# Gated-delta stage of a two-block network: the second chunk's decays and the work behind four value heads are traced one head later, and the transposes get two more PSUM banks

## The chip, the cores and the metric

The kernel runs on one core of a Trainium2 chip. The metric is the device time of one execution in microseconds (us), as the median over several runs. Beside it there is the profile of one execution, taken by the hardware profiler, whose rows are quoted below. Engines are named as in the profile: PE is the matrix engine (PEld its weight loads), DVE the vector engine, ACT the scalar engine, POOL the GpSimd engine, SP the queue that issues nearly all DMAs.

## The reference

The reference computes two blocks on 256 tokens of width 1024: a hybrid attention mixer with a product-key expert layer, and then a block of banded attention followed by a gated delta rule over 16 meta tokens and two chunks of 128 tokens. The change lies in the last part, which is this (cut to what matters):

```python
def deltanet_mixer(h, norm_w, w_in, conv_w, ...):
    u = rms_norm(h, norm_w) @ w_in
    qkv, z, b, a = split(u)
    qkv = silu(causal_depthwise_conv(qkv, conv_w))      # 4 taps
    q, k = l2_norm(...), l2_norm(...)                   # 8 key heads, 16 value heads
    beta, g = sigmoid(b), -exp(a_log) * softplus(a + dt_bias)
    o = chunked_gated_delta_rule(q, k, v, beta, g)
    return (rms_norm(o, o_norm_w) * silu(z)) @ w_out

def step(S, (qc, kc, vc, bc, gc)):                      # one chunk, per head
    gcum  = cumsum(gc)
    decay = exp(where(causal, gcum[:, None] - gcum[None, :], -inf))
    m     = where(strict, (kc * bc) @ kc.T * decay, 0)
    u, w  = solve(m + eye, [vc * bc, kc * bc * exp(gcum)])   # unit triangular
    v_new = u - w @ S
    o     = (qc * exp(gcum)) @ S + ((qc @ kc.T) * decay) @ v_new
    S     = S * exp(gcum[-1]) + (kc * exp(gcum[-1] - gcum)).T @ v_new
    return S, o
```

## The kernel before, in words

Everything is written for one core in a tile language. A scheduler takes the traced instructions and gives each engine a fixed list, in which it lets the earlier traced instruction go first among those that its own timeline holds ready; on the chip each engine then goes through its list from the front, and an instruction that waits holds back all behind it. Buffers of a pool are handed out in turn in the order of the trace: a tile that gets the buffer of an older one has to wait for the last reader of that one.

The delta stage (`delta`, from L1258) projects the input with 49 weight units of 128 x 1024. In this text they are numbered in order: unit 0 holds the gates b and a, units 1 to 8 the key heads, 9 to 16 the query heads, 17 to 32 the 16 value heads, 33 to 48 the 16 gate heads z. For each unit SP loads `raw` (L265, 4 buffers), ACT makes `hi` (L273, 3 buffers), DVE makes `lo` (L274, 3 buffers), and PE does 24 matmuls (L284 to L286) into `pj_ps`, a pool of two PSUM banks. So `hi` and `lo` of a unit need the buffers that PE frees when it is done with the unit three before, and PE's next unit needs a bank that ACT has read.

A head's convolution (`conv_head`, L1332) is two copies on ACT (`cpad`, and `craw` or `qT`: L1344, L1345) that free the bank, and three steps on DVE (L1356). Four value heads form one `raw` tile, called `craw` in the rows (2 buffers). When its four heads are done, ACT takes the SiLU of it (L1361), PE transposes it for the two chunks and for the meta tokens (`tp`, L1602, L1608, and the keys of the meta tokens L1613), ACT copies the results out (`v` L1604, `va` L1610, `ka` L1615), PE forms `mv` (L1618), DVE `vsA` (L1621), PE `mS`, and ACT the state `S` (L1626). All four `tp` banks of a group come from the pool `pb`, two banks, which `mv`, `mS` and the scores `kq` of `attend` use too. The tiles of z share the two buffers of `craw` (tag `craw`): the heads of the second z tile, units 37 to 40, are written over the last group's `raw`.

Two things run beside that. First the decays: for each chunk, `decay` sums the log decays on PE into four banks (`dec`, two from `pk` and two from `pb`), `between` adds the causal mask on PE (L1405) and takes 16 exponentials on ACT (L1409), DVE multiplies by the key products (`U`, L1500), and SP writes the 32 x 32 diagonal blocks of `U` to DRAM (`e1`, L1503). Second the inverse (`inverse`, a generator that `values` advances by one piece at each of its yields): SP reads all blocks back as 128 rows (`ab`, L1522), DVE solves them in 31 pairs of steps (`sb_t` L1253, `ub` L1255), SP writes the result (`e2`, L1527, named `e<-ub` in the rows) and reads it into the diagonal of `U` (L1530), and then, for each of 8 groups (2 chunks x 4 groups of heads), PE, ACT and DVE join the blocks in a chain: `r1` (L1550), `pr` on ACT (L1553), `zt` and `z1` (L1558, L1562), copies, `r2` (L1570), `rn` on ACT (L1573), `z2` (L1576). `zt` and `z2` use the two banks of `pk`, in turn.

After the last unit `step(0, h0)` and `step(1, h0)` run the recurrence itself, and `out` multiplies with the output weights.

Of the kernel before, what the change touches and what calls it, by code (L numbers as in the profile page):

```python
# [6 lines left out]
F32 = mybir.dt.float32  # L7
# [4 lines left out]
AF = mybir.ActivationFunctionType  # L12
ALU = mybir.AluOpType
# [5 lines left out]
M = 16  # L19
# [171 lines left out]
class Net:  # L191
# [1066 lines left out]
    def delta(self, NZ=2, AH=4, KN=8, SS=1, SR=3, SW=3):  # L1258
        nc, ap = self.nc, self.ap
        ident, tri = self.c("ident"), self.c("tri")  # L1260
# [5 lines left out]
        pb = self.pool("pb3", bufs=2, space=PSUM, side="left")  # L1266
        pj = self.pool("pj3", bufs=2, space=PSUM, side="right")
        pk = self.pool("pk3", bufs=2, space=PSUM, side="right")
        bank = lambda p, n: p.tile([128, 4, 128], F32, name=n, tag="b")
        flat = lambda x: x.rearrange("p a d -> p (a d)")  # L1270
        (hh, hl), R = self.hT, self.R
        V = self.pool("deV", side="right")
        W = self.pool("deW1", side="right")
        units = iter(range(49))
        CH = (slice(0, M), slice(M, M + 128), slice(M + 128, L))
# [23 lines left out]
        tp = bank(pb, "tp")  # L1299
# [11 lines left out]
        lb, g, gc, negc, bw = [sm(n) for n in ("lbeta", "gdec", "gcum", "negc2", "betaw")]  # L1311
# [20 lines left out]
        def conv_head(dst, b, t0=0):  # L1332

            n = L - t0
            t = max(t0 - 4, 0)
            w = [conv[:, b, i:i + 1] for i in range(4)]
            ps = proj(slice(t, L))
            src = W.tile([128, L], F32, name="cpad", bufs=2)[:, :L - t]
            early = 8 <= b < 8 + KN
            if early:  # L1340
                nc.vector.tensor_mul(src, ps, R)  # L1341
                ps = src
            else:
                nc.scalar.activation(src, ps, AF.Copy)  # L1344
            nc.scalar.activation(dst, ps[:, t0 - t:t0 - t + n], AF.Copy, scale=w[3])  # L1345
            for i in (2, 1, 0):

                o = max(3 - i - t0, 0)
                at = t0 - t - 3 + i + o
                x, y = src[:, at:at + n - o], dst[:, o:]  # L1350
                if early and i == 2:
                    x2 = W.tile([128, L], F32, name="ctap", bufs=2)[:, :n - o]
                    nc.scalar.activation(x2, x, AF.Copy, scale=w[i])
                    nc.gpsimd.tensor_add(y, y, x2)
                else:
                    nc.vector.scalar_tensor_tensor(y, x, w[i], y, op0=ALU.mult, op1=ALU.add)  # L1356

        def silu(raw, after=None, src=None):

            with self.tc.issue_after(self.last), self.tc.issue_after(after or self.last):  # L1360
                return nc.scalar.activation(raw, raw if src is None else src, AF.Silu).ins  # L1361
# [20 lines left out]
        kT = A.tile([128, 8, L], F32, name="kT")  # L1382
        qT = A.tile([128, 8, T], F32, name="qT", tag="q8")
        half = lambda n, c: A.tile([128, 16, 128], F32, name=f"{n}{c}", tag=f"{n}{c}")
        U = [half("U", c) for c in range(2)]
        at, qg = [[half(n, 0)] for n in ("at", "qg")]
        blocks = [slice(32 * b, 32 * b + 32) for b in range(4)]
        e1 = dr.tile([2, 4, 16, 32, 32], F32, name="e1")
# [14 lines left out]
        def between(c, h0, ps):  # L1403

            nc.tensor.matmul(flat(ps), self.causb, self.identb[:, None, :].to_broadcast([128, 4, 128]),  # L1405
                             start=False, stop=True, skip_group_check=True)
            for j in range(4):
                h = h0 + j
                self.last = nc.scalar.activation(at[c][:, h], ps[:, j], AF.Exp, bias=lb[:, c + 1, h:h + 1]).ins  # L1409

        def products(c, b):

            ps = bank(pa, "kk")
            for j in range(4):
                k = kT[:, 4 * b + j, CH[c + 1]]
                nc.tensor.matmul(ps[:, j], k, k, start=j == 0, stop=True, skip_group_check=True)
            return ps

        ss = W.tile([128, 3, 8], F32, name="ss")
        ri = A.tile([128, 3, 8], F32, name="rinv")  # L1420
# [35 lines left out]
        ps = pb.tile([128, 8, M], F32, name="mkk", tag="b")  # L1456
        for j in range(8):
            nc.tensor.matmul(ps[:M, j], kT[:, j, CH[0]], kT[:, j, CH[0]], start=j == 0, stop=True,
                             skip_group_check=True)
# [10 lines left out]
        a4 = am.rearrange("p (j r) c -> p j r c", r=2)  # L1470
# [5 lines left out]
        um = A.tile([M, 16, M], F32, name="um")  # L1476
# [6 lines left out]
        u4 = um.rearrange("p (j r) c -> p j r c", r=2)  # L1483
        nc.gpsimd.tensor_tensor(u4, u4, ri[:M, 0, :, None, None].to_broadcast([M, 8, 2, M]), op=ALU.mult)


        sums = {}
        for c in range(2):
            for h0 in range(0, 16, 4):
                sums[c, h0] = decay(c, h0)  # L1490
            kk = [products(c, b) for b in range(2)]
            for b in range(2):
                diagonal(ss[:, c + 1, 4 * b:4 * b + 4], kk[b], 128, 128)
            norms(c + 1, 128)
            for h0 in range(0, 16, 4):
                between(c, h0, sums[c, h0])
                u4 = U[c][:, h0:h0 + 4].rearrange("p (j r) c -> p j r c", r=2)
                a4 = at[c][:, h0:h0 + 4].rearrange("p (j r) c -> p j r c", r=2)
                j = h0 % 8 // 2
                nc.vector.tensor_tensor(u4, a4, kk[h0 // 8][:, j:j + 2, None, :].to_broadcast([128, 2, 2, 128]),  # L1500
                                        op=ALU.mult)
            for b, s in enumerate(blocks):
                nc.sync.dma_start(e1[c, b].rearrange("m s c -> s m c"), U[c][s, :, s])  # L1503

        def attend(c, h0):
            ts = CH[c + 1]
# [76 lines left out]
        S = A.tile([128, 16, 128], F32, name="S", tag="S")  # L1583
        v = []

        def values():
            for j in range(8):
                conv_head(qT[:, j], j, M)
            v.extend(half("v", c) for c in range(2))
            for h0 in range(0, 16, 4):  # L1590
                hs = slice(h0, h0 + 4)
                raw = A.tile([128, 4, L], F32, name="craw", bufs=2)
                for j in range(4):
                    conv_head(raw[:, j], 16 + h0 + j)
                    if h0 and j % 2:
                        attend(j // 2, h0 - 4)
                    yield
                silu(qT[:, h0 // 2:h0 // 2 + 2], silu(raw))
                for c in range(2):
                    tp = bank(pb, "tp")  # L1600
                    for j in range(4):
                        nc.tensor.transpose(tp[:, j], raw[:, j, CH[c + 1]], ident)  # L1602
                    for j in range(0, 4, 2):
                        nc.scalar.activation(v[c][:, h0 + j:h0 + j + 2], tp[:, j:j + 2], AF.Copy,  # L1604
                                             scale=ri[:, c + 1, (h0 + j) // 2:(h0 + j) // 2 + 1])
                tp = bank(pb, "tp")
                for j in range(4):
                    nc.tensor.transpose(tp[:M, j], raw[:, j, CH[0]], ident)  # L1608
                va = W.tile([M, 4, 128], F32, name="va")
                nc.scalar.activation(va, tp[:M], AF.Copy)  # L1610
                tp = bank(pb, "tp")
                for j in range(2):
                    nc.tensor.transpose(tp[:M, j], kT[:, h0 // 2 + j, CH[0]], ident)  # L1613
                ka = W.tile([M, 2, 128], F32, name="ka")
                nc.scalar.activation(ka, tp[:M, 0:2], AF.Copy)  # L1615
                ps = bank(pb, "mv")
                for j in range(4):
                    nc.tensor.matmul(ps[:M, j], um[:, h0 + j], va[:, j], start=True, stop=True,  # L1618
                                     skip_group_check=True)
                vs = W.tile([M, 4, 128], F32, name="vsA")  # L1620
                nc.vector.tensor_tensor(vs, ps[:M], bw[:M, 0, hs, None].to_broadcast([M, 4, 128]), op=ALU.mult)  # L1621
                ps = bank(pb, "mS")
                for j in range(2):
                    nc.tensor.matmul(flat(ps[:, 2 * j:2 * j + 2]), ka[:, j],
                                     flat(vs[:, 2 * j:2 * j + 2]), start=True, stop=True, skip_group_check=True)
                nc.scalar.activation(S[:, hs], ps, AF.Copy)  # L1626
            for c in range(2):
                attend(c, 12)
                yield
            for h0 in range(0, 4 * NZ, 4):  # L1630
                z = A.tile([128, 4, T], F32, name="z", tag="craw", bufs=2)
                yield from gates(z)
                sz.append(z)
            self.logexp()

        def gates(z):
            for j in range(4):
# [11 lines left out]
        W = self.pool("deW3", side="right")  # L1649
# [112 lines left out]
        op = [o0, o1]  # L1762
# [14 lines left out]
        for c in range(2):  # L1777
            for f in range(2):
# [5 lines left out]
                v = slice(a.stop, 512)  # L1784
# [32 lines left out]
```

## Time and profile before

| what | value |
|---|---|
| median of 3 runs | 1466.9 us (1466.56 to 1468.81) |
| profiled execution: its own time | 1468.61 us |
| profiled execution: span from first to last instruction | 1466.8 us |
| granted clock of PE, mean over the span | 0.997 |
| PE busy | 1438.7 us, 98% of the span |
| DVE busy | 1069.1 us, 73% |
| ACT busy | 793.1 us, 54% |

The delta stage lies between about 1164 us and the end. A row of the timeline gives start, duration, engine, line, output and inputs, how many instructions are merged in it, and in brackets how long the engine stood idle before it and what ended that. A row of the windows gives, for a stretch, the busy time of each engine with its number of instructions, the granted clock of PE, the share of the DMA engines and their rate.

### The profile page before, as it was taken

The numbers are of one execution on the slowest core, as the hardware profiler recorded it, in microseconds if no ns is written. First come the engines' busy times: TensorE is split into PE (matmuls) and PEld (weight loads), VectorE is DVE, ScalarE is ACT, GpSimd is POOL, SyncE is SP. The second block draws the span as 40 slices with busy tenths as digits, with TensorE's granted clock in tenths as the row PEclk, the third lists the DMA queues.
The fourth block names the chain that finished last, engine by engine and source line by source line (L and its number), as shares of the span: only waits on it lengthen the run. The fifth ranks groups of instructions, "written<-read, shape, count | busy, mean of one in ns | idle before, by whom it ended". The sixth has DMA issues, their size and how long they took to land.

```text
span 1466.8 us, 27081 instructions
## 1 busy us (share of the span) xinstructions
PE 1438.7 (98%) x10627; PEld 1323.2 (90%) x10627; DVE 1069.1 (73%) x2127; ACT 793.1 (54%) x1367; POOL 72.5 (5%) x106
## 2 busy tenths in 40 slices
PE   9999999999999999999999999999999989999998
PEld 9889999999999999999888888888898989899777
DVE  7667578789948888898555555555777698885576
ACT  5556544545544444444444445444686667664464
POOL 0000000000000000000000000000113024000020
PEclk9999999999999999999999999999999999999999
DMA  7453364555655555555666666666442444545113
GB/s 245 128 164 96 117 212 138 170 171 168 195 183 160 159 157 160 159 158 169 192 191 197 192 195 197 196 192 190 154 128 75 145 120 130 169 127 159 33 44 115
DMA packets 72223, 229.19 MB, mean 156 GB/s; under 512 B 16048, under 2 KB 16464, under 8 KB 72096
## 3 DMA queue, kind: packets, MB, share of 16 engines
q1 hardware_dynamic: 71408, 225.69, 50.2%
q8 instruction: 83, 1.36, 0.4%
q0 software_dynamic: 400, 1.46, 0.3%
q10 hardware_dynamic: 288, 0.33, 0.1%
q14 instruction: 44, 0.36, 0.1%
HBM read 225.31 MB, written 2.13 MB: 155 GB/s over the span
## 4 chain that ended last, share of the span: by engine, by line
PE 93%; ACT 3%; DVE 2%; issue 1%; DMA 0%; SPq 0%; POOL 0%; ACTq 0%; DVEq 0%
PE pu_ps L284 10%; PE pu_ps L285 9%; PE pu_ps L286 9%; PE acc L284 8%; PE acc L285 8%; PE acc L286 8%; PE pj_ps L284 8%; PE pj_ps L285 8%; PE pj_ps L286 8%; PE pt_ps L928 2%; PE tr_ps L370 1%; PE out L284 1%; PE out L285 1%; PE out L286 1%; ACT hi L273 1%
## 5 line engine op out<-in xcount | busy, mean ns | idle before, releaser
L273 ACT ACTIVATE hi<-raw 128x1024 fp32r<-128x1024 f32 x421 | 444.7, 1058 | 433.9 <-PE pu_ps L285 164.0
L274 DVE TENSOR_TENSOR lo<-raw,hi 128x1024 fp32r<-128x1024 f32 x421 | 517.3, 1230 | 196.1 <-ACT hi L273 195.0
L284 PE MATMUL pu_ps<-x2h,hi 128*128 128x256 f32 x1152 | 330.8, 288 | 0.5 <-ACT x2h L278 0.5
L285 PE MATMUL pu_ps<-x2l,hi 128*128 128x256 f32 x1152 | 326.4, 284 | 0.2 <-DVE x2l L279 0.2
L286 PE MATMUL pu_ps<-x2h,lo 128*128 128x256 f32 x1152 | 326.0, 283 | 0.2 <-DVE lo L274 0.2
L285 PEld LDWEIGHTS pu_ps<-x2l,hi 128*128 128x128 f32 x1152 | 221.0, 192 | 0.4 <-DVE x2l L279 0.4
L284 PEld LDWEIGHTS pu_ps<-x2h,hi 128*128 128x128 f32 x1152 | 220.5, 192 | 0.7 <-ACT x2h L278 0.7
L286 PEld LDWEIGHTS pu_ps<-x2h,lo 128*128 128x128 f32 x1152 | 220.7, 192 | 0.4 <-DVE lo L274 0.4
L285 PE MATMUL acc<-lo,ch 128*128 128x512 f32 x512 | 198.8, 389 | 0.0
L286 PE MATMUL acc<-hi,cl 128*128 128x512 f32 x512 | 198.2, 389 | 0.0
L284 PE MATMUL acc<-hi,ch 128*128 128x512 f32 x512 | 139.0, 389 | 0.0
L284 PE MATMUL pj_ps<-hh,hi 128*128 128x272 f32 (+1 forms) x424 | 122.0, 291 | 3.9 <-DVE cpad L1341 2.6
L285 PE MATMUL pj_ps<-hl,hi 128*128 128x272 f32 (+1 forms) x424 | 122.9, 291 | 0.7 <-DVE hl L330 0.6
L286 PE MATMUL pj_ps<-hh,lo 128*128 128x272 f32 (+1 forms) x424 | 123.1, 291 | 0.0
L286 PEld LDWEIGHTS acc<-hi,cl 128*128 128x128 f32 x512 | 96.1, 188 | 20.0
L285 PEld LDWEIGHTS acc<-lo,ch 128*128 128x128 f32 x512 | 96.1, 188 | 19.8
L284 PEld LDWEIGHTS acc<-hi,ch 128*128 128x128 f32 x512 | 96.0, 188 | 19.9
L284 PE MATMUL pj_ps<-nh,hi 128*128 128x256 f32 (+2 forms) x320 | 93.5, 292 | 1.8 <-ACT craw L1345 1.8
L285 PE MATMUL pj_ps<-nl,hi 128*128 128x256 f32 (+2 forms) x320 | 92.8, 290 | 0.0
L286 PE MATMUL pj_ps<-nh,lo 128*128 128x256 f32 (+2 forms) x320 | 92.1, 288 | 0.0
L284 PEld LDWEIGHTS pj_ps<-hh,hi 128*128 128x128 f32 x424 | 79.3, 188 | 5.7 <-issue 3.1
L285 PEld LDWEIGHTS pj_ps<-hl,hi 128*128 128x128 f32 x424 | 79.9, 188 | 2.0 <-DVE hl L330 1.1
(566 smaller groups left out, 2437.5 us busy)
## 6 DMA issues: line engine op xcount, KB each, us to landing
raw<-w_u SPq DMA_DIRECT2D x128, 512.0 KB, 3.7
raw<-w_v SPq DMA_DIRECT2D x128, 512.0 KB, 3.6
raw<-w_t SPq DMA_DIRECT2D x106, 512.0 KB, 3.7
raw<-w_o SPq DMA_DIRECT2D x32, 512.0 KB, 3.6
raw<-w_q SPq DMA_DIRECT2D x16, 512.0 KB, 3.7
raw<-w_br SPq DMA_DIRECT2D x8, 512.0 KB, 3.7
raw<-w_c SPq DMA_DIRECT2D x4, 512.0 KB, 3.7
xT<-xT SPq DMA_DIRECT2D x4, 256.0 KB, 5.2
```

What stands on the lines that cost most here:

```text
L273: nc.scalar.activation(hi, raw, AF.Copy)
L274: self.residual = (eng or nc.vector).tensor_sub(lo, raw, hi).ins
L284: mm(out, a[0], b[0], start=start, stop=False, **kw)
L285: mm(out, a[0], b[1], start=False, stop=False, **kw)
L286: mm(out, a[1], b[0], start=False, stop=stop, **kw)
L370: nc.tensor.transpose(tp[:, j], b, self.c("ident"))
L928: nc.tensor.matmul(ps[:, j], at[:, r, j // 2, :, j % 2], bt[:, j // 2, :, j % 2], start=j == 0 and r == 0, stop=r == 1, skip_group_check=True)
```

## The change: what it does

There are three edits, all in `delta`. First, the second half of the loop over chunks becomes a function `triangular(c, kk)`: `between`, `U`, and the write of the blocks. For the first chunk it is still called in the loop; for the second it is called inside `values`, behind the first value head (unit 17), before the first yield. Second, what follows four value heads becomes a function `natural(h0, raw)`, and is called behind the first head of the next group (for the last group directly after the loop, as before). Third, two of the four `tp` banks of `natural` now come from `pk` instead of `pb`: the one for the second chunk and the one for the keys.

```diff
-        sums = {}
-        for c in range(2):
-            ...
-            norms(c + 1, 128)
+        def triangular(c, kk):
             for h0 in range(0, 16, 4):
                 between(c, h0, sums[c, h0])
                 ...
             for b, s in enumerate(blocks):
                 nc.sync.dma_start(e1[c, b].rearrange("m s c -> s m c"), U[c][s, :, s])
+        sums = {}
+        for c in range(2):
+            ...
+            norms(c + 1, 128)
+            if c == 0:
+                triangular(c, kk)
...
+            made = None
             for h0 in range(0, 16, 4):
                 raw = A.tile([128, 4, L], F32, name="craw", bufs=2)
                 for j in range(4):
                     conv_head(raw[:, j], 16 + h0 + j)
+                    if h0 + j == 0:
+                        triangular(1, kk)
+                    if made:
+                        natural(*made)
+                        made = None
                     if h0 and j % 2:
                         attend(j // 2, h0 - 4)
                     yield
-                silu(qT[:, h0 // 2:h0 // 2 + 2], silu(raw))
-                ...
+                made = h0, raw
+            natural(*made)
...
+        def natural(h0, raw):
+            silu(qT[:, h0 // 2:h0 // 2 + 2], silu(raw))
             for c in range(2):
-                    tp = bank(pb, "tp")
+                tp = bank((pb, pk)[c], "tp")
             ...
-                tp = bank(pb, "tp")
+            tp = bank(pk, "tp")
             for j in range(2):
                 nc.tensor.transpose(tp[:M, j], kT[:, h0 // 2 + j, CH[0]], ident)
```

The next lists are pieces of the engines' fixed lists. First ACT, before, where the second chunk's 16 exponentials (`hh`) stand beside the first value heads' copies (`cpad`, `craw`):

```order
L1433 ACTIVATE rinv<-ss 128x8
L1409 ACTIVATE hh_13597<-dec,lbeta 128x128 x16
L1344 ACTIVATE cpad<-pj_ps 128x272
L1345 ACTIVATE craw<-pj_ps,dat_sb 128x272
L273 ACTIVATE hi<-raw 128x1024 x2
```

The same place on ACT after the change:

```order
L1433 ACTIVATE rinv<-ss 128x8
L1344 ACTIVATE cpad<-pj_ps 128x272
L1345 ACTIVATE craw<-pj_ps,dat_sb 128x272
L1409 ACTIVATE hh_13597<-dec,lbeta 128x128 x16
L273 ACTIVATE hi<-raw 128x1024
L1344 ACTIVATE cpad<-pj_ps 128x272
```

The two copies of unit 17 now stand ahead of the exponentials, those of unit 18 behind them, and one `hi` has moved from behind to before them (it stands above this piece).

Second PE, before, at the end of unit 38, where the last group's key transposes and `mv` stand (`Activation`, `DVE`, `Pool` and `DMAHW` are the semaphores that a row waits for):

```order
L286 MATMUL pj_ps<-nh_13149,lo 128x256
L1613 MATMUL tp<-cst,kT 16x128 [waits PE_49,Activation_49]
L1618 MATMUL mv<-va,um 16x128 [waits Activation_49]
L1618 MATMUL mv<-va,um 16x128 x3
L284 MATMUL pj_ps<-nh_13149,hi 128x256 [waits Activation_49]
```

The same place on PE after the change (`r`, `zt` and `z` are the first group of the inverse, `U_13226` the first chunk's matrix, `tp<-cst,craw` the second chunk's transposes of the last value heads; the last row is the first matmul of unit 39):

```order
L286 MATMUL pj_ps<-nh_13149,lo 128x256
L1642 MATMUL mv<-va,um 16x128 [waits Activation_49]
...
L1555 MATMUL r_14932<-pr,U_13226 32x32 [waits DMAHW0_49,DVE_49,Pool_49]
...
L1563 MATMUL zt<-pr,U_13226 32x32 [waits Activation_49]
...
L1575 MATMUL r_15039<-pr,U_13226 64x64 [waits Activation_49]
...
L1581 MATMUL z_15046<-U_13226,rn 64x64 [waits DMAHW1_49,Activation_49]
...
L1626 MATMUL tp<-cst,craw 128x128 x4
...
L1637 MATMUL tp<-cst,kT 16x128 [waits DVE_49]
...
L1563 MATMUL zt<-pr,U_13226 32x32 [waits PE_49,Activation_49]
...
L284 MATMUL pj_ps<-nh_13149,hi 128x256 [waits Activation_49]
```

Before, unit 39 follows `mv` directly, and the first `r` stands 86 matmuls of units (3.6 units) later, between heads; now the first group of the inverse stands between `mv` and unit 39.

Third DVE, before, behind the last group's `vsA`:

```order
L1253 TENSOR_TENSOR sb_t<-ub,ab 128x60
L1621 TENSOR_TENSOR vsA<-mv,betaw 16x512
L274 TENSOR_TENSOR lo<-raw,hi 128x1024
L1255 TENSOR_TENSOR ub<-ub,sb_t 128x30x2
L1253 TENSOR_TENSOR sb_t<-ub,ab 128x31
L1255 TENSOR_TENSOR ub<-ub,sb_t 128x31
L274 TENSOR_TENSOR lo<-raw,hi 128x1024
```

The same place on DVE after the change (of the twelve steps of the solve the first two and the last two):

```order
L1645 TENSOR_TENSOR vsA<-mv,betaw 16x512
L274 TENSOR_TENSOR lo<-raw,hi 128x1024
L1253 TENSOR_TENSOR sb_t<-ub,ab 128x156
L1255 TENSOR_TENSOR ub<-ub,sb_t 128x26x6
...
L1253 TENSOR_TENSOR sb_t<-ub,ab 128x31
L1255 TENSOR_TENSOR ub<-ub,sb_t 128x31
L1549 STREAM_TRANSPOSE pr<-U_13226 32x4x32 x7
```

Before, three steps of the solve are left behind the `lo` of unit 41; now there are twelve, and the transposes that feed the first `r` follow them without another `lo` between. On SP the write `e2` stands behind the load of unit 45 in both lists; the reads into `U` follow it now directly, where before the load of unit 46 stood between.

## Rows read from the trace of the kernel before

**Rows 1.** Waits of PE from 1150 us on: line, for whom, total us, times, longest

```profile
PE pj_ps L284 <- DVE cpad L1341: 2.6, 1, 2.6
PE pj_ps L284 <- ACT craw L1345: 1.8, 2, 1.5
PE tp L1613 <- ACT v L1604: 1.4, 1, 1.4
PE tp L1602 <- ACT craw L1361: 1.0, 1, 1.0
```

**Rows 2.** Windows: busy us of PE, PEld, DVE, ACT, POOL, PE's clock, DMA

```profile
1360.00:1370.00 10.00, 8.46 (x134) 6.68 (x133) 6.67 (x20) 4.84 (x10) 0.39 (x2) 1.00 0.32 102
1370.00:1380.00 10.00, 9.44 (x109) 7.97 (x106) 5.33 (x16) 4.45 (x11) 1.46 (x2) 1.00 0.01 3
```

**Rows 3.** Timeline of ACT at the second chunk's exponentials

```profile
1234.58 4.23 ACT L1409 ACTIVATE hh<-dec,lbeta 128x128 f32<-128x128 f32 x16 [0.72 <-DVE lbeta L1435]
```

**Rows 4.** Timelines of DVE and ACT before the first group's SiLU

```profile
1249.40 0.19 DVE L1253 TENSOR_TENSOR sb_t<-ub,ab 128x31 f32<-128x31 f32 x1 [2.72 <-DMA ab<-e]
...
1253.98 1.28 ACT L1361 ACT_TABLE_LOAD   x1 [0.97 <-DVE craw L1356]
```

**Rows 5.** Timeline of PE: the last group's `mv`, and the inverse's first `r`

```profile
1319.00 1.04 PE L1618 MATMUL mv<-va,um 16*16 16x128 f32 x8
...
1333.93 0.44 PE L1550 MATMUL r<-pr,U 128*32 128x32 f32 x14
```

**Rows 6.** Timeline of DVE: the end of the solve

```profile
1317.28 0.31 DVE L1255 TENSOR_TENSOR ub<-ub,sb_t 128x156 f32<-128x156 f32 x1
...
1319.49 0.22 DVE L1253 TENSOR_TENSOR sb_t<-ub,ab 128x60 f32<-128x60 f32 x1
1320.08 0.68 DVE L1621 TENSOR_TENSOR vsA<-mv,betaw 16x512 f32<-16x512 f32 x1 [0.37 <-PE mv L1618]
1320.68 1.20 DVE L274 TENSOR_TENSOR lo<-raw,hi 128x1024 fp32r<-128x1024 f32 x1
...
1322.30 0.22 DVE L1255 TENSOR_TENSOR ub<-ub,sb_t 128x31 f32<-128x31 f32 x1
```

**Rows 7.** Timeline of SP's DMA issues around the solve's way out and back

```profile
1317.39 4.86 SPq L265 DMA_DIRECT2D raw<-w_t  x2
1322.59 0.33 SPq L1527 DMA_DIRECT2D e<-ub  x1
...
1328.70 4.05 SPq L1530 DMA_DIRECT2D U<-e  x8
```

**Rows 8.** Time to landing: of L1527 (`e<-ub`), then of L1530 (`U<-e`)

```profile
DMA to landing us min/median/max: 6.1/6.1/6.1
...
DMA to landing us min/median/max: 1.9/2.3/2.4
```

**Rows 9.** DMA issues of the page: KB each, us to landing

```profile
raw<-w_t SPq DMA_DIRECT2D x106, 512.0 KB, 3.7
```

**Rows 10.** Timeline of ACT: the links of the inverse's chain, and two copies

```profile
1317.62 0.84 ACT L1604 ACTIVATE v<-tp,rinv 128x256 f32<-128x256 f32 x2 [1.51 <-PE tp L1602]
...
1318.82 0.36 ACT L1361 ACTIVATE z<-pj_ps 128x256 f32<-128x256 f32 x1
...
1334.47 0.56 ACT L1553 ACTIVATE pr<-r 32x128 f32<-32x128 f32 x2 [2.29 <-PE r L1550]
...
1340.80 0.38 ACT L1573 ACTIVATE rn<-r 64x256 f32<-64x256 f32 x1 [0.91 <-PE r L1570]
```

**Rows 11.** Windows of 1 us around two places where PE's clock falls

```profile
1133.00:1134.00 1.00, 0.65 (x3) 0.53 (x3) 1.00 (x3) 0.28 (x1) 0.00 (x0) 0.71 0.47 188
1134.00:1135.00 1.00, 1.00 (x6) 1.00 (x5) 0.02 (x1) 0.00 (x0) 0.00 (x0) 0.50 0.00 0
...
1136.00:1137.00 1.00, 1.00 (x7) 1.00 (x7) 0.00 (x0) 0.00 (x0) 0.00 (x0) 0.58 0.00 0
...
1464.00:1465.00 1.00, 0.00 (x0) 0.00 (x0) 0.00 (x0) 0.00 (x0) 0.00 (x0) 0.76 1.01 355
```

More of the change, by code (lines that the diff above doesn't have):

```diff
@@ L1484, in delta @@
         nc.gpsimd.tensor_tensor(u4, u4, ri[:M, 0, :, None, None].to_broadcast([M, 8, 2, M]), op=ALU.mult)
-        sums = {}
-        for c in range(2):
[L1489 to L1493, printed above, removed]
-            norms(c + 1, 128)
+        def triangular(c, kk):
             for h0 in range(0, 16, 4):
@@ L1503, in delta @@
                 nc.sync.dma_start(e1[c, b].rearrange("m s c -> s m c"), U[c][s, :, s])
+        sums = {}
+        for c in range(2):
+            for h0 in range(0, 16, 4):
+                sums[c, h0] = decay(c, h0)
+            kk = [products(c, b) for b in range(2)]
+            for b in range(2):
+                diagonal(ss[:, c + 1, 4 * b:4 * b + 4], kk[b], 128, 128)
+            norms(c + 1, 128)
+            if c == 0:
+                triangular(c, kk)
         def attend(c, h0):
@@ L1589, in values @@
             v.extend(half("v", c) for c in range(2))
+            made = None
             for h0 in range(0, 16, 4):
-                hs = slice(h0, h0 + 4)
                 raw = A.tile([128, 4, L], F32, name="craw", bufs=2)
@@ L1597, in values @@
                     yield
-                silu(qT[:, h0 // 2:h0 // 2 + 2], silu(raw))
-                for c in range(2):
-                    tp = bank(pb, "tp")
[L1601 to L1605, printed above, removed]
-                tp = bank(pb, "tp")
[L1607 to L1626, printed above, removed]
+                made = h0, raw
+            natural(*made)
             for c in range(2):
@@ L1634, in values @@
             self.logexp()
+        def natural(h0, raw):
+            hs = slice(h0, h0 + 4)
+            silu(qT[:, h0 // 2:h0 // 2 + 2], silu(raw))
+            for c in range(2):
+                tp = bank((pb, pk)[c], "tp")
+                for j in range(4):
+                    nc.tensor.transpose(tp[:, j], raw[:, j, CH[c + 1]], ident)
+                for j in range(0, 4, 2):
+                    nc.scalar.activation(v[c][:, h0 + j:h0 + j + 2], tp[:, j:j + 2], AF.Copy,
+                                         scale=ri[:, c + 1, (h0 + j) // 2:(h0 + j) // 2 + 1])
+            tp = bank(pb, "tp")
+            for j in range(4):
+                nc.tensor.transpose(tp[:M, j], raw[:, j, CH[0]], ident)
+            va = W.tile([M, 4, 128], F32, name="va")
+            nc.scalar.activation(va, tp[:M], AF.Copy)
+            tp = bank(pk, "tp")
+            for j in range(2):
+                nc.tensor.transpose(tp[:M, j], kT[:, h0 // 2 + j, CH[0]], ident)
+            ka = W.tile([M, 2, 128], F32, name="ka")
+            nc.scalar.activation(ka, tp[:M, 0:2], AF.Copy)
+            ps = bank(pb, "mv")
+            for j in range(4):
+                nc.tensor.matmul(ps[:M, j], um[:, h0 + j], va[:, j], start=True, stop=True,
+                                 skip_group_check=True)
+            vs = W.tile([M, 4, 128], F32, name="vsA")
+            nc.vector.tensor_tensor(vs, ps[:M], bw[:M, 0, hs, None].to_broadcast([M, 4, 128]), op=ALU.mult)
+            ps = bank(pb, "mS")
+            for j in range(2):
+                nc.tensor.matmul(flat(ps[:, 2 * j:2 * j + 2]), ka[:, j],
+                                 flat(vs[:, 2 * j:2 * j + 2]), start=True, stop=True, skip_group_check=True)
+            nc.scalar.activation(S[:, hs], ps, AF.Copy)
         def gates(z):
```

## The prediction

> **What bounds the kernel now.** I read the page first: PE is busy for 98% of the span, so time can only be won where PE stands still, and is lost where it is made to. Then the waits of PE in the delta stage, then the timelines around each of them. Between unit 17 and the last z head PE stands still three times, 4.2 us together [rows 1]: 1.5 for a bank of `pj_ps`, 1.3 for a SiLU and the bank behind it (1.0 and 0.3), 1.4 for a `tp` bank. The first has its cause on ACT, where the copies of unit 17 stand behind 16 exponentials of 4.23 us [rows 3]. The second begins on DVE: its first solve step waited 2.72 us for the read `ab`, the taps of the convolution queued up behind it, and ACT began the first SiLU, with a table load of 1.28, only at 1253.98 [rows 4]. After the last unit another 2.1 us are idle in 20 us, in small waits between the inverse's steps and the recurrence's [rows 2]. The inverse itself is hidden: `mv` of the last group runs at 1319.00, the first full `r` at 1333.93, and the 14 us between are filled with 86 matmuls of units; `r` waited for nothing [rows 5]. What PE does in those 14 us is the cover of a long path that is not PE's: the solve on DVE, its way to DRAM, and back.
>
> **The change part by part.** No arithmetic is added or removed; about the same PE work stands in another order.
>
> *The exponentials behind unit 17.* ACT now frees unit 17's bank first; unit 18's copies stand behind the 4.23 us and one `hi` of some 1.1 instead. Until unit 20 asks for that bank PE has units 18 and 19 to do, 48 matmuls; at the pace of [rows 5] (86 in under 14 us with what stands between, 0.16 each) that is at most 7.7 us, against 4.23 + 1.1 + some 0.8 for the copies, 6.1. I take 0.2 of the 1.5 as left (0 to 1).
>
> *The work behind four heads, one head later.* The blocks of the second chunk are written later by the same step, so `ab` lands later too: in the list its first reader on DVE stands in front of two taps of unit 20. I expect the same kind of wait there as the 2.72 us, and the SiLU stands behind unit 21's copies as before. But the transposes stand 0.8 of a unit into the next head but one, so PE meets it later. I take 0.6 of 1.3 as left (0 to 2).
>
> *Two more banks.* The keys' transposes no longer wait for the copy of `v`; I take 0.2 of 1.4 as left. The three together: 4.2 less 1.0 is a gain of 3.2 (1.5 to 4.2).
>
> *What the two banks cost.* This is the large term. The two `tp` of the last group now get `pk` banks in turn with `zt` and `z2` of the inverse, and in trace order the first group's `zt` and `z2` come before them. So the second chunk's transposes of the last group must wait until the inverse has begun; the z heads of units 37 and 38 can't be copied out before that, since they go into that group's `raw`; both `pj_ps` banks are then full, and unit 39 can't start. The changed PE list has exactly this: behind `mv` at the end of unit 38 stands the first `r`, and unit 39 comes after `zt`, `z2`, the transposes and a wait for ACT. The cover of 14 us is gone. What is left between the end of `mv` and `r`: `vsA` 0.60 to the next start, `lo` of unit 41 and, in the changed DVE list, twelve steps of the solve behind it. `lo` and the last three of them took 1.84 here (1320.68 to 1322.52), the seven from the 156-column `ub` to the 60-column `sb_t` 2.21, two more about 0.35 each [rows 6]: 4.75. None of it can start earlier, because `vsA` waits for `mv`. Then `e<-ub`, which took 6.1 to land, and `U<-e`: eight issues in 4.05, so the fourth, the last of chunk 0, is issued 1.5 after the first and lands 2.3 later: 3.8 [rows 7, 8]. In the 6.1 I see a queue: the second of the two `raw` loads before it ended its issue at 1322.25, was issued about 1321.9 and needs 3.7 [rows 9], which is 1325.6; `e<-ub` landed 3.1 later, at 1328.7. In the changed order that load is issued when `lo` of unit 41 is done, 2.9 us ahead of `e<-ub` and more, so it is all but landed. I take 3.1 (bounds: 1.9, the shortest landing of `U<-e`, and 6.1). Wait of PE: 0.60 + 4.75 + 0.1 + 3.1 + 3.8 = 12.3 (11.1 to 15.3).
>
> *The chain in front of unit 39.* Behind the first `r` come `pr` 0.56, the `zt` copy, `rn` 0.38, `v` 0.84 and `z` 0.36 on ACT [rows 10], some 2.4 with the `zt` copy, and between them seven groups of small matmuls of PE, each some 0.44 to 0.6 by that of `r` [rows 5], 3 to 4. About 0.7 of ACT's links lies beside the next group's `r` and `z`, so the whole takes some 5.5 and I take 1.7 of it as idle (1 to 3); the small matmuls are moved, not new.
>
> *The clock.* In the us from 1133 on, with PE 0.65 busy, the granted clock fell to half, and it came back only between 1136 and 1137, though PE was fully busy from 1134 on: 0.29 + 0.5 + 0.5 + 0.42, 1.7 us lost. It fell again in the us from 1464 on, where no matmul is left [rows 11]. I expect the lower level, 1.2 GHz, to hold through the chain (5.5 us, of which some 1 is lost) and through as much of the dense matmuls behind it as there (1.7 lost): 2.7 (0 to 5). The Trainium skill (TensorE: Matmul & The Clock Gate, Part 1: The HAM clock gate) says that half rate is the state without activity and that activity releases it; here the trace agrees, with 0.50 in the us behind a thin stretch. By that rule alone the term stays, without it the sum is 2.7 less.
>
> *ACT's tables.* In the changed list the table for Exp and Ln is loaded among the z heads and the SiLU's loaded again: one more load of 1.28 [rows 4], partly beside PE. I take 0.5 (0 to 1.5).
>
> *Given back later.* In the changed list most of the inverse and the first recurrence steps stand between units 39 to 48. Of the 2.1 us of small waits [rows 2] I take 1.5 as gone (0 to 2.5).
>
> Sum: 12.3 + 1.7 + 2.7 + 0.5 − 3.2 − 1.5 = 12.5 us slower. The profiled execution took 1468.61 us, span 1466.8 plus 1.8 around it; by that I expect 1481.1 there. It lies 1.7 above the median of the runs shown, 1466.9; measured medians should give 1466.9 + 12.5 = 1479.4.
>
> **The rivals.**
> - *The way back is as slow as before.* `e<-ub` takes 6.1 us whatever is ahead of it, and the clock stays low longer since the chain's groups keep PE thin: 15.3 + 2.5 + 4 + 0.5 − 3.2 − 1.5 = 17.6, 1484.5. For it speaks the only measured landing; against it the load that stood just in front.
> - *The clock stays.* All as forecast without its 2.7: 1476.7. For it: PE's longest wait of the stage, 2.6 us [rows 1], falls in no window of a lower clock; but it is a fifth of this one.
> - *The return is hidden after all*, and the kernel is faster. Place: `r` behind `mv`. If `U` were back when PE comes there, there would be no wait and no fall of the clock, and only gains stay: 4.2 + 2.1, 1460.6. It decides from a wait of some 4 us down. Against it: DVE's twelve steps stand behind `vsA`, and that waits for this same `mv`.
> - *A draw.* The wait shrinks to some 5 us and the gains pay for it: 1467. The solve alone is 5.4 of the 12.3, so both landings would have to be nothing, where 1.9 is the least that one took [rows 8].
> - *The early edits do nothing* (each of the three waits comes back at another place), with the new wait as forecast: 12.5 + 3.2 = 15.7, 1482.6.
>
> **How the numbers follow.** Forecast 0.45; slow way back 0.20; early edits nothing 0.10; the clock stays 0.15; hidden 0.05; a draw 0.05. What a measurement can tell from no change is some 0.2%, 2.9 us. So faster 0.05, same 0.05, slower 0.90. All least terms give 11.1 + 1 − 4.2 − 2.5 = +5.4; all worst 15.3 + 3 + 5 + 1.5 − 1.5 = +23.3. The range leaves out the hidden case, the draw and the ends where all terms agree: 1472 to 1486.
>
> **What the profile will show.** One wait of PE of 11 to 15 us before an `r` matmul, released by a DMA or by DVE's transposes, around 1316 to 1330, and idle windows with a clock of 0.5 behind it. No wait for `tp` of the keys on a copy of `v`, and none of 1.46 behind the exponentials. `e<-ub` landing in about 3 us. What stands behind the last unit starts some 12 us later, and the last stage is as long as before. I am wrong if `r` waits less than 5 us, if the solve's last step comes before the last group's `vsA`, or if unit 39 runs before `r`.

## The result, and the profile after

The changed kernel takes 1475.3 us (median, 1473.0 to 1477.7), the kernel before 1466.9 (1464.7 to 1468.8) in runs beside it: a ratio of 1.0058, 95% interval 1.0045 to 1.0070, some 8.4 us slower. The forecast was 1479.4, with 1472 to 1486 as its range. The profiled execution took 1474.08 us, with a span of 1472.3 and a mean granted clock of 0.992.

First the waits of PE from 1228 to 1400 us, after the change:

```profile
PE r L1555 <- DMA U<-e: 10.8, 1, 10.8
PE pj_ps L284 <- ACT craw L1345: 0.6, 1, 0.6
PE r L1555 <- DVE pr L1549: 0.5, 1, 0.5
PE zt L1563 <- ACT pr L1558: 0.4, 1, 0.4
```

The three stalls of [rows 1] are down to 0.6 us, both waits for `tp` are gone, and there is one new wait of 10.8 us. The timeline of PE shows where it stands, and what lies between it and unit 39 (last row):

```profile
1311.69 1.04 PE L1642 MATMUL mv<-va,um 16*16 16x128 f32 x8
1323.55 0.28 PE L1555 MATMUL r<-pr,U 128*32 128x32 f32 x2 [10.81 <-DMA U<-e]
1324.33 0.62 PE L1555 MATMUL r<-pr,U 128*32 128x32 f32 x14 [0.50 <-DVE pr L1549]
...
1326.43 1.11 PE L1575 MATMUL r<-pr,U 64*64 64x64 f32 x8
...
1329.08 1.11 PE L1626 MATMUL tp<-cst,craw 128*128 128x128 f32 x4
...
1331.79 0.58 PE L284 MATMUL pj_ps<-nh,hi 128*128 128x256 f32 x1
```

Against [rows 5]: between `mv` and the full `r` there were 86 matmuls of units, now there is none. The next rows are DVE's (first four) and SP's of the same time, and the landing of `e<-ub`:

```profile
1312.77 0.68 DVE L1645 TENSOR_TENSOR vsA<-mv,betaw 16x512 f32<-16x512 f32 x1 [0.23 <-PE mv L1642]
1313.38 1.20 DVE L274 TENSOR_TENSOR lo<-raw,hi 128x1024 fp32r<-128x1024 f32 x1
...
1317.81 0.21 DVE L1255 TENSOR_TENSOR ub<-ub,sb_t 128x31 f32<-128x31 f32 x1
1322.63 0.49 DVE L1549 STREAM_TRANSPOSE pr<-U 32x128 f32<-32x128 f32 x2 [4.61 <-DMA U<-e]
```

```profile
1318.10 0.33 SPq L1532 DMA_DIRECT2D e<-ub  x1
1320.72 4.04 SPq L1535 DMA_DIRECT2D U<-e  x8
```

```profile
e<-ub SPq DMA_DIRECT2D x1, 512.0 KB, 2.6
```

The chain can be read off: `mv` ends at 1312.73; `vsA` takes 0.6 up to the start of `lo`; `lo` and twelve solve steps end at 1318.02; `e<-ub` takes 2.6 to land (6.1 in [rows 8]); and from the first issue of `U<-e` to the first `r` it is 2.8. The 1 us windows of that stretch have PE's busy time in the second column and the clock in the third from last:

```profile
1315.00:1316.00 1.00, 0.00 (x0) 0.00 (x0) 0.90 (x4) 0.00 (x0) 0.00 (x0) 1.00 0.74 66
1316.00:1317.00 1.00, 0.00 (x0) 0.00 (x0) 0.90 (x4) 0.00 (x0) 0.00 (x0) 0.54 0.71 287
...
1332.00:1333.00 1.00, 1.00 (x5) 1.00 (x6) 0.47 (x2) 0.23 (x1) 0.00 (x0) 0.50 0.00 0
1333.00:1334.00 1.00, 1.00 (x10) 1.00 (x9) 0.00 (x0) 0.00 (x0) 0.00 (x0) 0.93 0.00 0
```

The clock stays at its lower level, 1.2 GHz, from 1316 to 1333, 1.3 us into unit 39. Later the inverse stands between units, and the small waits of [rows 2] are gone:

```profile
1360.00:1370.00 10.00, 10.00 (x98) 9.33 (x98) 5.42 (x12) 4.67 (x9) 0.20 (x1) 1.00 0.38 114
1370.00:1380.00 10.00, 10.00 (x106) 9.33 (x105) 4.88 (x11) 4.76 (x8) 1.46 (x2) 1.00 0.28 91
```

Single executions differ ahead of the delta stage, so stretches are compared from the first matmul of unit 9, the first that reads `nh`, to the first `out<-hi,o0h`. The rows that give the starts and the ends (the first of the two times of a row), before and then after:

```profile
L284 PE MATMUL pj_ps<-nh,hi x320: 275/284/471, 1194.8 to 1360.2; 128*128 128x272 f32 x64, 128*128 128x256 f32 x64, 128*128 128x260 f32 x32
...
L284 PE MATMUL out<-hi,o0h x32: 392/395/483, 1402.0 to 1459.6; 128*128 128x512 f32 x32
```

```profile
L284 PE MATMUL pj_ps<-nh,hi x320: 276/283/582, 1193.0 to 1382.5; 128*128 128x272 f32 x64, 128*128 128x256 f32 x64, 128*128 128x260 f32 x32
...
L284 PE MATMUL out<-hi,o0h x32: 389/396/483, 1407.7 to 1465.0; 128*128 128x512 f32 x32
```

That is 207.2 us before and 214.7 after: 7.5 longer. The table gives this stretch for all kernels, with PE's idle time in it (windows of 2 us summed; "early" is the first 118 us) and the time at half clock (from the clock of the same windows), all from the one profiled execution of each kernel; the last columns are the timed runs.

| kernel | stretch | idle | of it early | at half clock | median | ratio to before, interval |
|---|---|---|---|---|---|---|
| before | 207.2 | 7.0 | 4.3 | 0 | 1466.9 | |
| after | 214.7 | 13.0 | 0.6 | 17.1 | 1475.3 | 1.0058, 1.0045 to 1.0070 |
| e1, all banks from pb | 204.6 | 5.3 | 2.3 | 0 | 1464.9 | 0.9983, 0.9968 to 0.9999 |
| e2, banks alone | 216.8 | 15.0 | 2.6 | 17.0 | 1477.2 | 1.0058, 1.0036 to 1.0080 |
| e3, last group pb | 203.9 | 3.6 | 0.9 | 3.4 | 1463.3 | 0.9969, 0.9954 to 0.9985 |
| e4, SW 5 | 202.3 | 3.3 | 0.7 | 0 | 1462.3 | 0.9963, 0.9949 to 0.9977 |
| e5, fill | 214.6 | 4.7 | 1.5 | 6.8 | 1474.3 | 1.0045, 1.0029 to 1.0060 |
| e6, without edit 1 | 204.2 | 5.5 | 2.5 | 0 | 1465.5 | 0.9984, 0.9973 to 0.9996 |
| e7, without edit 2 | 202.4 | 3.6 | 0.7 | 0 | 1463.1 | 0.9969, 0.9958 to 0.9979 |
| e8, SW 4 | 215.8 | 14.0 | 1.1 | 17.1 | 1476.9 | 1.0066, 1.0051 to 1.0080 |
| e9, fill of small matmuls | 217.9 | 2.0 | 0.6 | 20.5 | 1478.9 | 1.0082, 1.0069 to 1.0095 |
| e10, short solve | 203.8 | 2.4 | 0.6 | 6.8 | 1463.9 | 0.9978, 0.9969 to 0.9987 |
| e11, SW 5 without edit 2 | 201.9 | 3.2 | 0.6 | 0 | 1462.6 | 0.9966, 0.9954 to 0.9978 |
| e12, fill of transposes | 214.5 | 3.9 | 0.6 | 6.8 | 1475.4 | 1.0059, 1.0045 to 1.0072 |

### The profile page after: what moved, and what is told of

Its sections match the earlier page's. It is cut to its first block, busy times and chain, and to the rows that moved or that the text cites. A ratio compares the mean times of both kernels' runs of the same rounds, so it can differ in the third digit from the quotient of the medians.

```text
span 1472.3 us, 27069 instructions
## 1 busy us (share of the span) xinstructions
PE 1438.0 (98%) x10627; PEld 1323.9 (90%) x10627; DVE 1069.0 (73%) x2127; ACT 794.1 (54%) x1368; POOL 73.1 (5%) x106
## 4 chain that ended last, share of the span: by engine, by line
PE 92%; DVE 3%; ACT 2%; issue 1%; DMA 1%; POOL 0%; SPq 0%; ACTq 0%; DVEq 0%
PE pu_ps L284 9%; PE pu_ps L285 9%; PE pu_ps L286 9%; PE acc L284 8%; PE pj_ps L284 8%; PE pj_ps L286 8%; PE acc L285 8%; PE acc L286 8%; PE pj_ps L285 8%; PE pt_ps L928 2%; PE tr_ps L370 1%; PE out L284 1%; PE out L285 1%; PE out L286 1%; PE sc_ps L681 1%
```

## The experiments

**Is it the banks?** Theory: the pk banks put the inverse's first group ahead of the last group's transposes, hence ahead of unit 39. Rival: the later place of `natural` does it. Four kernels take the two apart.

e1, both moves with the old banks:

```diff
-                tp = bank((pb, pk)[c], "tp")
+                tp = bank(pb, "tp")
...
-            tp = bank(pk, "tp")
+            tp = bank(pb, "tp")
```

> The changed kernel with all four tp banks from pb again; the two moves of edit 1 and 2 stay. My theory (the shared pk banks tie the last group's transposes to the inverse): the 10.8 us wait before r goes, and the half-clock stretch behind it; the exponentials' stall stays removed, the 1.4 us wait of the keys' transposes is back. Before less about 2.4: 1464.5 (1462.5 to 1466.5), PE's longest wait in the stage under 3 us. Rival A (the later place of the work behind four heads delays unit 39): still 1474 to 1476 with a wait of about 10 us.

It took 1464.9. The longest wait before the first `r` is 0.3, and PE's longest wait in the stretch is 1.1, that of the keys' `tp`, which is back:

```profile
PE tp L1637 <- ACT v L1628: 1.1, 1, 1.1
```

e2 is the reverse, the old order with the third edit alone:

```diff
-                    tp = bank(pb, "tp")
+                    tp = bank((pb, pk)[c], "tp")
...
-                tp = bank(pb, "tp")
+                tp = bank(pk, "tp")
             for j in range(2):
```

> The kernel before with the third edit alone: two of the four tp banks from pk. My theory: the same wait of 9 to 12 us before the first r, the clock at 0.50 behind it, and none of the early gain but the tp bank's: 1475 to 1481, taken 1478. Rival A (the moves are the cause, not the banks): 1465 to 1467, and no wait above 3 us.

It took 1477.2, and its longest wait of PE is the one of the changed kernel:

```profile
PE r L1550 <- DMA U<-e: 10.9, 1, 10.9
```

So the third edit alone makes the loss, and the loss needs neither of the moves. It is 1.9 slower than the changed kernel, about the early idle time that it keeps (2.6 against 0.6 in the table). e3 takes the pk banks away from the last group only:

```diff
-                tp = bank((pb, pk)[c], "tp")
+                tp = bank((pb, pk)[c if h0 < 12 else 0], "tp")
...
-            tp = bank(pk, "tp")
+            tp = bank(pk if h0 < 12 else pb, "tp")
```

> The changed kernel, where only the last group of heads takes all its tp banks from pb; the first three groups keep the two pk banks. My theory: no long wait, and the early gain of 3.6 us whole: 1463.3 (1462 to 1465). Rival A (the moves cause the wait): 1474 to 1476. Rival B (the early edits give nothing by themselves, only the order of the units changes): 1466 to 1468.

It took 1463.3, as the theory had it, with no wait over 0.2 before the first `r`: of the third edit only the last group's transposes, those of the second chunk and those of the keys, make the wait. e4 keeps all banks and starts the inverse's groups two pieces later:

```diff
-    def delta(self, ..., SR=3, SW=3):
+    def delta(self, ..., SR=3, SW=5):
```

> The changed kernel with the inverse's first group begun two pieces later (SW 5 instead of 3), so that zt and z2 of the first group get their banks behind the last group's transposes; all four tp banks as in the changed kernel. My theory (what counts is who is first in the turn of the pk banks): no wait above 3 us before r, 1463 to 1467, taken 1464.5, part of it spent where the inverse now ends two pieces later. Rival C (sharing pk with the inverse costs by itself, in whatever order): still 1473 to 1477.

It took 1462.3. Sharing `pk` costs nothing that shows here; who is traced first decides. The waits of PE from 1228 to 1400 in e4 begin with:

```profile
PE z L1581 <- ACT rn L1578: 0.9, 2, 0.5
PE pj_ps L284 <- ACT craw L1345: 0.6, 1, 0.6
```

e8 (`SW=4`) asks whether it is the order or the number of banks: only `zt` is then traced ahead of the transposes, and by the turn of the pool the other bank is left to them.

> The changed kernel with the inverse begun one piece later (SW 4): zt of its first group is traced ahead of the last group's transposes, z2 behind them, so that one of the two pk banks is free when the second chunk's transposes ask for it. Theory 1 (the order of the trace decides: a tile of the pool gets no bank before those traced ahead of it have got theirs; r stands right behind mv in PE's list, as in the changed kernel): again a wait of 9 to 12 us before r, clock 0.50, 1472 to 1476, taken 1474. Theory 2 (what counts is that both banks are taken): no wait over 3 us, 1462 to 1465.

```profile
PE r L1555 <- DMA U<-e: 11.2, 1, 11.2
```

```profile
1328.64 0.29 PE L1563 MATMUL zt<-pr,U 128*32 128x32 f32 x2
1328.87 1.12 PE L1626 MATMUL tp<-cst,craw 128*128 128x128 f32 x4
```

The wait is back in full, and the transposes run directly behind the first `zt`. That speaks for the order, since a free bank did not help them; that the bank was free follows from the trace of the program, and no row shows it. The time, 1476.9, is 0.9 over the range given.

**What do the moves give?** e6 and e7 are e3 with one move undone:

```diff
             if c == 0:
-                triangular(c, kk)
+            triangular(c, kk)
...
-                    if h0 + j == 0:
-                        triangular(1, kk)
```

> e3_last_pb (1463.3) with the first edit undone: the second chunk's exponentials stand ahead of the first value head again. My theory: PE's wait of 1.5 us for the bank of pj_ps is back in place of 0.6, and the time is 1463.3 + 0.9 = 1464.2 (1463.5 to 1465.5). Rival F (the whole early gain comes from the first edit): 1466 to 1467. Rival G (the first edit gives nothing): 1463.3, and the wait of 1.5 is not there.

It took 1465.5; two of the old waits return, the first of the size it had in [rows 1], the second as there:

```profile
PE pj_ps L284 <- ACT craw L1345: 1.5, 1, 1.5
PE tp L1623 <- ACT craw L1361: 1.0, 1, 1.0
```

e7 calls `natural` at the end of its own group again:

```diff
-                    if made:
-                        natural(*made)
-                        made = None
...
-                made = h0, raw
-            natural(*made)
+                natural(h0, raw)
```

> e3_last_pb (1463.3) with the second edit undone: the work behind four value heads stands at the end of its own group again; triangular stays moved, the first three groups keep the two pk banks. My theory: the waits for a SiLU (1.0 to 1.3) are back, 0.3 there now: 1464.2 (1463.5 to 1465.5). Rival G2 (the second edit gives nothing by itself): 1463.3 with no such wait over 0.5. Rival H (it is the second edit that makes the gain, since natural's transposes then find everything ready): 1466 to 1467.

It took 1463.1, with an early idle time of 0.7: neither wait comes back. So the first edit removes both the bank's and the SiLU's wait (2.5 of early idle without it, 0.7 to 0.9 with it), the banks remove the keys' wait (early idle of e1 less that of e3: 1.4), and the second edit gives nothing that shows.

The same pair shows the clock at work in another place. The profiled execution of e3, unlike that of e7, has a fall of the clock in the later groups of the inverse:

```profile
1355.00:1357.00 2.00, 1.52 (x46) 1.26 (x36) 1.82 (x7) 0.72 (x3) 0.20 (x1) 0.97 0.36 61
1357.00:1359.00 2.00, 2.00 (x11) 1.70 (x10) 0.59 (x2) 1.75 (x3) 0.00 (x0) 0.50 0.50 201
1359.00:1361.00 2.00, 1.54 (x26) 0.77 (x25) 1.16 (x5) 0.27 (x1) 0.00 (x0) 0.68 0.00 0
```

Its stretch is 1.5 us longer than e7's with the same 3.6 of idle time, for 3.4 us at half clock. In the timed runs the two lie only 0.2 apart: the stretch is that of one execution, and not every execution of a kernel has such a fall.

**Is it the way back that `r` waits for?** e10 leaves out 12 of the 31 pairs of solve steps:

```diff
-            for s, _ in enumerate(self.subst(ub, ab, 32, V, nc.vector)):
+            steps = self.subst(ub, ab, 32, V, nc.vector)
+            for s in range(31):
+                if s < 19:
+                    next(steps)
```

> The changed kernel with 12 of the 31 pairs of solve steps left out (part of the computation is left out); banks and PE's order as in the changed kernel, r still directly behind mv. The solve is then done ahead of the last group's vsA, and U is back before PE comes to r. My theory (r waits for the solve and its way through DRAM; the shared banks only put r in unit 39's way): no wait over 1.5 us before r, the clock falls later or not at all, what is left of the cost is the idle time of the chain, 1 to 3 us: 1475.3 - 10.8 - 1.5 = 1463 (1461.5 to 1466). Rival I (the chain in front of unit 39 and the thin stretch's clock cost as much as the wait): 1467 to 1471.

It took 1463.9. Banks and PE's order are those of the changed kernel, but `r` follows `mv` at once, and the chain still stands in front of unit 39 (7.6 us from the first `r` to unit 39, 8.2 in the changed kernel):

```profile
1311.76 1.04 PE L1645 MATMUL mv<-va,um 16*16 16x128 f32 x8
1312.73 0.25 PE L1558 MATMUL r<-pr,U 128*32 128x32 f32 x2
1313.16 0.41 PE L1558 MATMUL r<-pr,U 128*32 128x32 f32 x14 [0.19 <-DMA U<-e]
```

```profile
1315.00:1316.00 1.00, 0.52 (x8) 0.39 (x7) 0.92 (x4) 0.38 (x1) 0.20 (x1) 1.00 0.97 401
1316.00:1317.00 1.00, 0.92 (x20) 0.88 (x21) 0.60 (x2) 0.28 (x2) 0.00 (x0) 0.60 0.69 193
...
1323.00:1324.00 1.00, 1.00 (x10) 0.99 (x8) 0.00 (x0) 0.00 (x0) 0.00 (x0) 0.98 0.00 0
```

That is 11.4 us less than the changed kernel, so what `r` waits for is the solve and its way back. The clock fell all the same, with no wait in front of the chain, for 6.8 us. Against e11 (below), which has no such fall, the stretch is 1.9 longer with 0.8 less idle, so I estimate the fall at some 2.7. The comparison is not clean: DVE has less to do in e10, and the groups stand elsewhere.

**Can the clock be held?** Three kernels fill the wait with work whose result nobody reads. e5 puts 72 transposes behind `mv`:

```diff
             ps = bank(pb, "mS")
+            if h0 == 12:
+                for i in range(72):
+                    nc.tensor.transpose(ps[:, i % 2], kT[:, i % 8, CH[1]], ident)
```

> The changed kernel with 72 more transposes of keys on PE between mv and the first r of the inverse (into the bank that mS overwrites afterwards; nothing of the result changes), which fill about 10 of the 10.8 us in which PE stood still. Nothing on the way back of the inverse is shortened. My theory (the fall of the granted clock is a cost of its own, 2.7 us in the prediction): the clock stays at 1.00 between 1312 and 1335, r waits under 2 us, the small matmuls behind it take half their time, and the whole takes 1472.6 (1471 to 1473.5). Rival D (the chain in front of unit 39 is bound by ACT and DVE, so PE's clock costs nothing there): 1475.3 (1474.5 to 1476.5) with the clock at 1.00. Rival E (thin work of PE keeps the clock low all the same): clock 0.50 behind the fill.

It took 1474.3: the clock was 1.00 through the fill, and fell behind it, in the chain (rival E). The fill also moved `kq` and a first `o` in front of `r`, with two waits of 0.8, so e9 and e12 fill from behind `vsA`, in the bank of `mv`. e9 does it with small matmuls:

```diff
+            if h0 == 12:
+                for i in range(38):
+                    nc.tensor.matmul(ps[:M, i % 4], um[:, h0 + i % 4], vs[:, i % 4], ...)
             ps = bank(pb, "mS")
```

> The changed kernel with 38 more matmuls of the form of mv (they read vsA and write the bank of mv, which nobody reads any more; the result doesn't change). They begin when vsA is done and fill some 10 us up to r and between its first matmuls; unlike e5_fill nothing else moves in PE's list. My theory (the fall of the clock costs 2.7 us): the granted clock stays at 1.00 from 1312 to 1335, and the time is 1475.3 - 2.7 = 1472.6 (1471 to 1473.6). Rival D (the chain in front of unit 39 is bound by ACT and DVE): clock at 1.00, but 1475.3 (1474.3 to 1476.3). Rival E (the thin chain takes the clock down by itself, as behind the fill of e5_fill): clock 0.50 a few us into the chain, 1474 to 1475.

It took 1478.9, slower than the changed kernel, which no theory had. The windows show PE busy without a gap, and the clock falls in the same us in which it fell with PE idle:

```profile
1315.00:1316.00 1.00, 1.00 (x12) 0.84 (x10) 0.90 (x4) 0.00 (x0) 0.00 (x0) 1.00 0.00 0
1316.00:1317.00 1.00, 1.00 (x9) 0.71 (x7) 0.90 (x4) 0.00 (x0) 0.00 (x0) 0.64 0.98 197
1317.00:1318.00 1.00, 1.00 (x6) 0.71 (x5) 0.86 (x5) 0.00 (x0) 0.00 (x0) 0.50 0.79 307
```

```profile
1313.79 11.93 PE L1648 MATMUL mv<-vsA,um 16*16 16x128 f32 x66 [0.77 <-DVE vsA L1645]
1325.65 0.32 PE L1555 MATMUL r<-pr,U 128*32 128x32 f32 x2
```

At half clock the fill grew to 11.93 us (its row counts 66 records, two for each matmul; the last five matmuls stand between the first steps of the inverse) and held `r` up itself. So it says nothing of the clock's price. e12 has 84 transposes of 128 x 128 in the same place (the edit is shown against e9):

```diff
-                for i in range(38):
-                    nc.tensor.matmul(ps[:M, i % 4], um[:, h0 + i % 4], vs[:, i % 4], ...)
+                for i in range(84):
+                    nc.tensor.transpose(ps[:, i % 4], kT[:, i % 8, CH[1]], ident)
```

> The changed kernel with 84 transposes of keys (128 x 128) in place of the 38 small matmuls of e9_fill2, behind vsA and into the same bank of mv, which nobody reads any more; the result doesn't change and nothing else in PE's list moves. They take some 9.4 us and end just ahead of r. My theory (e9's clock fell because of what its matmuls were, not because PE stood still, and the chain behind the fill takes the clock down by itself, as without any wait in e10): the clock stays at 1.00 through the fill, falls some us into the chain and is back at about the same place of unit 39; the first r to r2 is faster by some 0.4 us and the whole by about 1: 1474.3 (1473 to 1475.5). Rival K (what counts is only that PE has anything to do; e9 fell for another reason): clock 0.50 through the fill as in e9, 1478 to 1480. Rival L (the fall of the clock costs its 2.7 us, and the fill prevents it): 1472.6, clock 1.00 through the chain.

```profile
1315.30 9.39 PE L1648 MATMUL mv<-cst,kT 128*128 128x128 f32 x84 [0.77 <-DVE vsA L1645]
1325.61 0.22 PE L1555 MATMUL r<-pr,U 128*32 128x32 f32 x2 [0.93 <-DMA U<-e]
```

```profile
1317.00:1318.00 1.00, 1.00 (x12) 1.00 (x11) 0.90 (x4) 0.00 (x0) 0.00 (x0) 1.00 0.70 111
...
1328.00:1329.00 1.00, 0.91 (x8) 0.91 (x8) 0.57 (x2) 0.04 (x1) 0.00 (x0) 0.50 0.06 9
```

The clock held through the fill and fell in the chain, and the time is the changed kernel's (1475.4): rivals K and L are out. The low clock during the wait itself cost nothing that shows. What is left for it to cost is the chain and the 1.3 us of unit 39, and a fill of the wait does not reach that far. No kernel kept the clock at 1.00 through the chain, so its price there is an estimate.

**The best version.** e11 is the first and third edits with SW 5: the changed kernel with the edit of e7 and that of e4.

> The candidate for the best: the first and third edits (the second undone) with the inverse begun two pieces later, so that all four groups use the two pk banks and none stands behind the inverse. If the second edit gives nothing: as e4_sw5 and e7_no_edit2, 1462.5 (1461.5 to 1463.5). If the second edit gives something that e3 and e7 did not show: 1464 to 1465.

It took 1462.6. e3, e4, e7 and e11 lie within 1 us and are not told apart. The fastest median is e4's, 1462.3, with a ratio to before of 0.9963 (0.9949 to 0.9977), some 4.8 us under the runs of before beside it (1467.1): the changed kernel with one number altered.

## Why the prediction was right, and where its sizes were off

- *The step that decides* (the `pk` banks put `r`, with the solve and its way back, in front of unit 39) was right, and is shown from both sides: e1, e3 and e4 lose the wait, e2 and e8 have it, and e10 loses it with the banks as they are when the solve ends sooner. Three details held too: twelve solve steps behind `vsA`, `e<-ub` faster than its 6.1, the low clock behind the wait.
- *The wait*, forecast at 12.3 (11.1 to 15.3), was 10.8, below its lower bound. The 0.6 and 4.75 on DVE were right (vsA's start to the last step: 5.25). The landing took 2.6, not 3.1. The rest is the way back: the forecast waited for the fourth issue, 3.8, but the first `r` begins 2.8 after the first issue, and the next matmuls wait 0.5 more. I had priced the whole group where the first matmul needs only part of it.
- *The chain in front of unit 39*: its idle time, forecast at 1.7, was 0.9 in the two waits shown. The chain itself is longer than I took it for, 8.2 us (1323.55 to 1331.79) instead of 5.5; most of that is matmuls that are moved, not new.
- *Its clock*, forecast at 2.7, is not settled. After against e11 leaves 3.1 (12.8 longer, 9.7 more idle, before rounding), but after against before leaves only 1.6 (7.5 longer, 5.9 more idle). The single executions speak for the larger figure: over the 76 timed runs of the kernel before that stood beside e1 to e12, the time is 1.04 us longer for each 0.001 that the mean granted clock is lower (1464.9 at 1.000, 1474.2 at 0.991). As 0.001 of some 1467 us is 2.9 us at half clock, that is some 0.35 per us at half clock, and 3.4 for the 9.6 us from the first `r` to 1333.14; it is an estimate, since what lowers the clock can itself cost time. The loss is spread otherwise than forecast: 1.3 us at half in unit 39 where I took the loss of [rows 11], and more in the chain (`r2` 1.11 where e10's at full clock took 0.68).
- *The early stalls* gave 3.6 (idle 4.3 to 0.6), forecast 3.2, but one reason was wrong: I gave the SiLU's wait to the second edit and left 0.6 of it; it is the first edit that removes it, whole (e6, e7). Of the wait for the bank 0.6 is left, not 0.2.
- *Given back later*: the idle time behind the wait fell by some 2.2, forecast 1.5. *ACT's extra table load*, forecast at 0.5, ended no wait of PE.
- *The sum* of what was found, with 3.1 for the clock: 10.8 + 0.9 + 3.1 − 3.6 − 2.2 = 9.0, where the stretch measured 7.5. The 1.5 between them stay open: e1, e4, e6, e7 and e11, which have no fall of the clock, are also 0.9 to 1.5 shorter against before than their idle time explains.
- *The rivals.* "Slow way back" fell with the 2.6, "a draw" with the 10.8, "early edits nothing" with the early waits. "The clock stays" came near the time (1476.7) for a wrong reason. "Hidden" is what e10 shows when the solve ends in time, at 1463.9 rather than 1460.6. Of the signs that the profile was to show, one did not come: what stands behind the last unit starts 7.5 later, not some 12.

## What to carry to other kernels

When two stages share a pool, ask which of them is traced first and what the first waits for: a bank that is free for most of the time still chains the later stage to the earlier one's slowest input. Before giving a stage more banks, walk the engine's list at the last iteration, where the next stage begins; the fix may be to start that stage one step later rather than to give the banks back. In a sum over a chain, price the first instruction's own input, not the whole transfer. And work that nobody reads, put into a wait to hold the clock, gained nothing that shows here (e5, e12), or lost (e9): the clock fell again in the thin chain behind it.

## What the runs showed of the hardware

- PE's granted clock fell to 0.50 while PE was busy for 1.00 of each us, with matmuls of 16 x 16 weights (e9). With 128 x 128 transposes in the same place it stayed at 1.00 (e12), and it fell in the inverse's chain, where PE had been busy for 0.42 to 0.88 of each us, without any wait in front (e10). The Trainium skill (TensorE: Matmul & The Clock Gate, Part 1: The HAM clock gate) says that the gate is set by how busy PE has been. In e9 and e12 the profile's busy share alone did not tell which way the clock went.
- The spread of single executions goes with the granted clock: over 76 timed runs of the kernel before, from 1464.9 us at 1.000 to 1474.2 at 0.991, with a correlation of −0.97.
- The same write `e<-ub` of 512 KB took 6.1 us to land with two loads of 512 KB issued just ahead [rows 7, 8]; 5.1 in e10, issued 0.1 us behind the last load's issue; 4.8 in e1, 1.2 behind; and 2.6 to 3.4 where it was 1.4 us or more (e4 3.4, e3 2.6, e9 3.3, the changed kernel 2.6).
